# Seven block products for tiles 3 to 10 of the first feed-forward, with its modulation rows taken one token group at a time

## The chip, the cores and the metric

The kernel runs on one core of a Trainium2 chip. The metric is the device time of one execution in microseconds (us), as the median of several runs; lower is better. The profile is one further execution, taken by the hardware profiler.

The engines are named as in the profile: PE does the matrix products, DVE is the vector engine, ACT the scalar engine, POOL the general-purpose engine, SP the engine that only issues transfers. ACT can issue transfers too.

## The reference

One layer of a streaming encoder for 1024 prompt tokens and 32 sample tokens, which share all weights. The two token groups differ in the conditioning vector `c`, from which nine modulation rows of 1024 values each are made.

```python
def layer(x, c, ...):
    mod = (silu(c) @ w_ada + b_ada).reshape(B, 9, 1024)[:, None]
    modulate = lambda h, k: h * (1.0 + mod[:, :, 3*k+1]) + mod[:, :, 3*k]
    gate     = lambda k: 1.0 + mod[:, :, 3*k+2]

    f = swiglu(modulate(x, 0), ffn1_w1, ffn1_w3, ffn1_w2)      # 1024 -> 2816 -> 1024
    x = layer_norm(ALPHA * x + 0.5 * gate(0) * f, ...)
    proj = modulate(x, 1) @ w_in                               # then RG-LRU and spatial gating
    ...
    x = layer_norm(ALPHA * x + gate(1) * m, ...)
    f = swiglu(modulate(x, 2), ffn2_w1, ffn2_w3, ffn2_w2)
    x = layer_norm(ALPHA * x + 0.5 * gate(2) * f, ...)

def swiglu(h, w1, w3, w2):
    return (silu(h @ w1) * (h @ w3)) @ w2
```

So the first feed-forward needs rows 0 and 1 at its beginning (scale and shift) and row 2 (the gate) when its first result is added to `x`. Rows 3 to 8 are not needed before it ends.

## The kernel before

**Layout.** Activations lie transposed: 128 features on the partitions, tokens along the free axis, in three chunks of 384, 384 and 288 columns (`CH`). Every 32-bit operand of a matrix product is split into a rounded high part and a low rest, and a product is three matmuls: high by high, high by low, low by high. Weights are loaded by SP as 128x1024 tiles named `raw` (five buffers, 512 KB a load); ACT rounds the high part into a `wh` tile and DVE (for some pieces POOL) subtracts to get the low part. `wh` is a ring of eight. The order of all weight pieces is fixed by `stream_order`; `w_rel` hands a piece's place in the ring on as soon as PE has used it.

**The feed-forwards.** The 2816 hidden features are 22 tiles of 128, in blocks: [0, 1, 2], eight pairs [3, 4] to [17, 18], and [19, 20, 21]. For each block the hidden values g of its tiles are made first (below: H), then the down projection `F` adds all of the block's tiles to `x`. F works through its eight output tiles m, the first two together and then one by one, each with one PSUM bank per chunk (there are eight banks). `add_gated` on DVE multiplies a bank with the gate `gt` of row 2 and adds it to `x`, which also frees the bank. So a late `gt`, or a DVE that is behind, stops PE as soon as the banks are used up.

A plain tile (`H`) takes 8 input slices, 3 chunks, 2 weights (w1 and w3) and 3 matmuls each: 144 matmuls. A tile in the set `FAST` is done by `H_fast`: for the two chunks of 384 columns, the two weights and two halves of the input are taken as a 2 by 2 block product that needs seven block products in place of eight (Strassen's scheme in Winograd's form), 84 matmuls in place of 96; the third chunk stays plain (48). It pays with vector work: POOL makes four differences and sums of weight blocks per tile (in `w_source`) and splits three of the pieces, DVE adds intermediate results `y0`, `y1`, `z1` out of PSUM. A tile holds up to six PSUM banks and all five buffers `s` of intermediate values.

The seven products also need four combinations T1 to T4 of the input, once for a whole feed-forward. `combs` makes T1 and T3 (four steps of five instructions each, on POOL in the first feed-forward), then T2, which overwrites a part of the input and so waits until no plain tile needs that any more (`b12_free`); `comb_last` makes T4 behind the F that follows. T2 and T4 are made by DVE. T1 and T3 lie in the two `tx` buffers, T4 in the two `t4` buffers.

In the first feed-forward tiles 11 to 21 are fast, in the second tiles 3 to 21.

**The modulation rows.** Rows 0 and 1 are made by PE at the start. The other seven are made by `ada_rest` on DVE: per row eight weight tiles (`araw`, 128x1024), and for each of them one product with SiLU(c) of each token group (`cb`), multiplied and summed along the free axis in one instruction. A weight tile is loaded once (by SP) and used twice, first into a scratch tile `prod` (tag `acc`), then in place. The two `cb` lie in the `t4` buffers. Row 2 comes first.

**The order of work.** PE runs in program order. For DVE, ACT and POOL a scheduler orders the instructions by their place in the program and by when it reckons them ready. Side work is written as Python generators which are stepped while the matrix products are written out: `self.pe` adds up the estimated PE time (columns / 2.4 ns per matmul), and `yield 2.6` means that the generator goes on 2.6 us of PE time later. `drain` runs a generator to its end at once. `tc.issue_after(i)` puts instructions of an engine behind instruction i of that engine. Inside an engine everything runs in order: an instruction that waits holds all behind it.

`softplus` (some 30 tiny DVE instructions and one of POOL for the recurrent part) follows the first feed-forward in the program, queued behind the last instruction of the modulation rows.

Line numbers that the profile uses: L152 all matmuls; L209 and L210 high and low part of any split; L239 to L245 weight combinations on POOL; L561 and L562 other small work; L693 and L700 loads of `araw` and `cb`; L713 the modulation product; L722 `gt`; L767 to L770 the steps of T1 to T4; L817 the additions of a fast tile; L924 `add_gated`; L1160 to L1182 softplus.

Of the kernel before, what the change touches and what calls it, by code (L numbers as in the profile page):

```python
# [19 lines left out]
P = 128  # L20
# [30 lines left out]
FAST = {1: range(11, FF), 2: range(3, FF)}  # L51
# [72 lines left out]
class Core:  # L124
    def __init__(self, tc, ins, outs):
# [9 lines left out]
        self.window = False  # L135
        self.ln_out = {}
# [151 lines left out]
    def run(self):  # L288
# [396 lines left out]
    def ada_rest(self):  # L685
        nc, V = self.nc, self.nc.vector
        b_ada = self.v("b_ada").rearrange("p (m k) -> p m k", m=9)
        raws = {}

        def raw(n):  # L690
            if n < 56 and n not in raws:
                r = self.wpool.tile([P, 1024], F32, tag="raw", name="araw", bufs=RAWS)
                nc.sync.dma_start(r, self.i["ada1"][n])  # L693
                raws[n] = r


        cb = []
        for v in range(2):
            t = self.apool.tile([P, 4, 384], F32, tag="t4", name="cb", bufs=2).rearrange("p a b -> p (a b)")[:, 0:D]
            nc.sync.dma_start(t, self.i["crow"][v].partition_broadcast(P))  # L700
            nc.scalar.activation(t, t, AF.Silu)
            cb.append(t)
        raw(0)
        yield 1.0
        for m in range(2, 9):
            w = 1.8 if m == 2 else 2.6
            for f in range(K):
                n = (m - 2) * K + f
                raw(n)
                r = raws.pop(n)  # L710
                for v in range(2):
                    p = self.gpool.tile([P, D], F32, tag="acc", name="prod", bufs=1) if v == 0 else r
                    V.scalar_tensor_tensor(p, r, 1.0, cb[v], ALU.mult, ALU.mult, accum_out=self.mod[:, m, f, v:v + 1])  # L713
                    yield w
                    raw(n + 1)
            mod = self.mod[:, m, :, :]
            self.late = V.tensor_tensor(mod, mod, b_ada[:, m, :].unsqueeze(2).to_broadcast([P, K, 2]), ALU.add)
            self.mods.add(m)
            s = m // 3
            if m % 3 == 2:  # L720
                f = 0.5 if s != 1 else 1.0
                V.tensor_scalar(self.gt[:, s, :, :], mod, f, f, ALU.mult, ALU.add)  # L722
            if m % 3 == 1:
                self.coef(s, self.v("ln_g", (s - 1) * 8, s * 8), self.v("ln_b", (s - 1) * 8, s * 8), m, m - 1, 0, K)
                self.resid_coef(s, self.v("ln_g", (s - 1) * 8, s * 8), self.v("ln_b", (s - 1) * 8, s * 8))
# [20 lines left out]
    def g_tag(self, nf, t):  # L746
        return ("tx" if nf == 1 else "t4") if t == 2 else "tx" if t == LAST[2] else "g"
# [28 lines left out]
    def combs(self, e):  # L776
# [12 lines left out]
        while not self.b12_free:  # L789
            yield 1.0  # L790
        self.T2 = B12
# [10 lines left out]
    def H_fast(self, nf, t, later=False):  # L802
# [13 lines left out]
        def add(out, x, ps):  # L816
            V.tensor_tensor(out, x, ps[:, :n], ALU.add)  # L817
# [30 lines left out]
        self.w_rel(1)  # L848
        w = get("S3")
# [68 lines left out]
    def add_gated(self, ps, s, pc, m, tot=None):  # L918
# [4 lines left out]
        for (o, w, v) in segs(pc):  # L923
            V.scalar_tensor_tensor(X[:, m, a + o:a + o + w], ps[:, o:o + w], self.gt[:, s, m, v:v + 1],  # L924
                                   X[:, m, a + o:a + o + w], ALU.mult, ALU.add)
# [30 lines left out]
    def F(self, nf, block):  # L956
# [3 lines left out]
        for h in range(2):  # L960
            ws = [self.w_get((f"f{nf}w2", t, h)) for t in block]

            for ms in ((0, 1), (2,), (3,)) if h == 0 else ((0,), (1,), (2,), (3,)):
# [5 lines left out]
                for m in ms:  # L969
                    for c in range(3):  # L970
                        self.add_gated(ps[m][c], s, PIECES[c], 4 * h + m)
# [600 lines left out]
```

## Time and profile before

| | before |
|---|---|
| median of 3 runs | 1904.93 us (1904.32 to 1906.21) |
| the profiled execution | 1902.73 us |
| its span | 1901.0 us |
| mean granted PE clock | 0.991 |
| PE busy | 1847.3 us |
| DVE, ACT, POOL busy | 1257.2, 654.5, 443.7 us |
| first feed-forward, tile 1 to the F before the last block | 78 to 710 us |
| transfers | 141.08 MB, 74 GB/s over the span |
| `araw` loads | 56 of 512 KB, 3.2 us from issue to landing |
| `raw<-wst` loads (weights) | 156 of 512 KB, 3.3 us |

The span is the time from the first to the last instruction of the profiled execution; the execution's own time is 1.7 us longer. Busy times of the engines overlap, so they don't add up to the span. A row of instructions in the profile gives line, engine, operation, the tile written and the tiles read (`out<-in`), the shape, the count, and behind a bar the busy time and the mean of one; then the time that the engine stood idle before them and who ended it (`<-DMA araw<-ada` is the landing of a load).

### The profile page before, as it was taken

To read this page: it belongs to the slowest core of one execution; us is meant where nothing else is said; L and a number is where in the kernel's file an instruction comes from. 1 tells how busy PE (TensorE), PEld (TensorE's weight loads), DVE (VectorE), ACT (ScalarE), POOL (GpSimd) and SP (SyncE) were. 2 spreads that over 40 slices of the span, in tenths; PEclk is the share of its full clock that TensorE was granted. 3 is DMA by queue.
4 is the path that set the end of the run, shared out by engine and by line. 5 is a ranking of instruction groups with operands and counts; after the bars stand their busy time and mean duration, and the time that the engine had idled before them with its cause. 6 is when DMAs were issued, how large, how long until landed. Compare 5 with 4: busy or idle time off the path is not lost.

```text
span 1901.0 us, 28144 instructions
## 1 busy us (share of the span) xinstructions
PE 1847.3 (97%) x11402; PEld 1808.9 (95%) x11402; DVE 1257.2 (66%) x2307; ACT 654.5 (34%) x1144; POOL 443.7 (23%) x348
## 2 busy tenths in 40 slices
PE   6999999999999999989999999999999999999996
PEld 3899999999999999989789999999999999999996
DVE  6888878877554554873977466965645564555477
ACT  5641121112233223354554437232232233223324
POOL 2244200013233424022000000134233333423410
PEclk9999999999999999999999999999999999999998
DMA  7444344321112011222011401110121112111102
GB/s 281 145 156 135 124 152 133 123 89 41 49 45 67 23 52 60 85 77 81 3 53 45 158 23 45 45 58 32 45 67 45 45 45 67 36 54 46 45 1 92
DMA packets 39442, 141.08 MB, mean 74 GB/s; under 512 B 4368, under 2 KB 7056, under 8 KB 38544
## 3 DMA queue, kind: packets, MB, share of 16 engines
q1 hardware_dynamic: 37392, 130.03, 20.5%
q10 hardware_dynamic: 1920, 9.24, 1.2%
q8 instruction: 90, 1.47, 0.3%
q14 instruction: 40, 0.33, 0.1%
HBM read 130.52 MB, written 8.73 MB: 73 GB/s over the span
## 4 chain that ended last, share of the span: by engine, by line
PE 81%; DVE 10%; DMA 2%; ACT 1%; issue 1%; POOL 0%; POOLq 0%; DVEq 0%; ACTq 0%
PE ps L152 79%; DMA araw<-ada 2%; DVE araw L713 1%; DVE prod L713 1%; PE psl L152 1%; DVE xa L924 1%; DVE wh L210 1%; PE psz L152 1%; PE psg L152 0%; DVE g L210 0%; DVE tot L930 0%; DVE xb L1049 0%; ACT t L538 0%; DVE s L674 0%; DVE t L1060 0%
## 5 line engine op out<-in xcount | busy, mean ns | idle before, releaser
L152 PE MATMUL ps<-xh,wh 128*128 128x384 f32 (+1 forms) x4080 | 966.5, 320 | 2.3 <-ACT xh L545 1.8
L152 PEld LDWEIGHTS ps<-xh,wh 128*128 128x128 f32 x4080 | 709.4, 188 | 5.2 <-ACT xh L545 2.0
L152 PE MATMUL ps<-xl,wh 128*128 128x384 f32 (+1 forms) x2040 | 652.0, 320 | 3.3 <-DVE xl L548 3.2
L209 ACT ACTIVATE wh<-raw 128x512 fp32r<-128x512 f32 x420 | 262.1, 629 | 651.8 <-PE ps L152 553.1
L152 PE MATMUL ps<-g,wh 128*128 128x384 f32 (+1 forms) x2880 | 472.8, 324 | 4.3 <-DVE g L210 3.0
L152 PEld LDWEIGHTS ps<-g,wh 128*128 128x128 f32 x2880 | 464.0, 188 | 8.6 <-DVE g L210 4.5
L152 PEld LDWEIGHTS ps<-xl,wh 128*128 128x128 f32 x2040 | 384.2, 188 | 6.4 <-DVE xl L548 5.3
L210 DVE TENSOR_TENSOR wh<-raw,wh 128x512 fp32r<-128x512 f32 x283 | 200.4, 714 | 269.5 <-ACT wh L209 267.7
L210 POOL TENSOR_TENSOR wh<-raw,wh 128x512 fp32r<-128x512 f32 x137 | 196.2, 1433 | 331.1 <-ACT wh L209 330.8
L924 DVE SCALAR_TENSOR_TENSOR xb<-ps,gt,xb 128x384 f32<-128x384 f32 (+1 forms) x352 | 152.3, 486 | 84.9 <-PE ps L152 70.4
L924 DVE SCALAR_TENSOR_TENSOR xa<-ps,gt,xa 128x384 f32<-128x384 f32 (+2 forms) x320 | 136.6, 484 | 24.7 <-PE ps L152 24.2
L152 PE MATMUL ps<-tx,wh 128*128 128x384 f32 x720 | 129.8, 336 | 0.0
L152 PEld LDWEIGHTS ps<-tx,wh 128*128 128x128 f32 x720 | 124.3, 188 | 0.0
L209 ACT ACTIVATE g<-s 128x384 fp32r<-128x384 f32 x129 | 62.7, 493 | 170.2 <-DVE s L674 170.1
L239 POOL TENSOR_TENSOR raw<-raw 128x512 f32<-128x512 f32 x30 | 42.7, 1424 | 304.9 <-DVE wh L210 300.2
L210 DVE TENSOR_TENSOR g<-s,g 128x384 fp32r<-128x384 f32 x129 | 86.1, 674 | 20.8 <-ACT g L209 19.5
L817 DVE TENSOR_TENSOR s<-s,ps 128x384 f32<-128x384 f32 x120 | 66.3, 552 | 44.3 <-PE ps L152 44.3
L713 DVE SCALAR_TENSOR_TENSOR prod<-araw,cb 128x1024 f32<-128x1024 f32 x56 | 72.1, 1287 | 32.7 <-DMA araw<-ada 32.4
L669 ACT ACTIVATE s<-ps 128x384 f32<-128x384 f32 (+1 forms) x102 | 46.2, 453 | 120.7 <-PE ps L152 120.2
L562 POOL TENSOR_TENSOR r<-r,half 128x3 f32<-128x3 f32 x8 | 7.4, 924 | 308.1 <-DVE r L561 308.1
L713 DVE SCALAR_TENSOR_TENSOR araw<-araw,cb 128x1024 f32<-128x1024 f32 x56 | 74.2, 1325 | 1.2
L152 PE MATMUL ps<-T,wh 128*128 128x384 f32 x360 | 68.0, 337 | 0.0
(234 smaller groups left out, 1608.2 us busy)
## 6 DMA issues: line engine op xcount, KB each, us to landing
raw<-wst SPq DMA_DIRECT2D x156, 512.0 KB, 3.3
araw<-ada SPq DMA_DIRECT2D x56, 512.0 KB, 3.2
wnat<-ada SPq DMA_DIRECT2D x8, 512.0 KB, 9.9
raw<-ada SPq DMA_DIRECT2D x8, 512.0 KB, 3.4
xt<-x SPq DMA_DIRECT2D x7, 512.0 KB, 8.1
sp<-xa ACTq DMA_DIRECT2D x2, 1536.0 KB, 5.0
xb<-sp ACTq DMA_DIRECT2D x2, 1536.0 KB, 10.8
y<-xb SPq DMA_DIRECT2D x4, 768.0 KB, 3.5
```

The costliest lines, as they stand in the source:

```text
L152: self.nc.tensor.matmul(out, a, b, start=start, stop=stop, skip_group_check=True)
L209: self.nc.scalar.activation(dst_h, src, AF.Copy)
L210: (e or self.nc.vector).tensor_tensor(dst_l, src, dst_h.bitcast(F32), ALU.subtract)
L239: G.tensor_tensor(a["A21"], a["A11"], a["A21"], ALU.subtract)
L562: self.nc.gpsimd.tensor_tensor(out, out, self.half[:n, :w], ALU.pow)
L669: self.nc.scalar.activation(s, x[:, :n], AF.Silu)
L713: V.scalar_tensor_tensor(p, r, 1.0, cb[v], ALU.mult, ALU.mult, accum_out=self.mod[:, m, f, v:v + 1])
L817: V.tensor_tensor(out, x, ps[:, :n], ALU.add)
L924: V.scalar_tensor_tensor(X[:, m, a + o:a + o + w], ps[:, o:o + w], self.gt[:, s, m, v:v + 1], X[:, m, a + o:a + o + w], ALU.mult, ALU.add)
```

## The change

- `FAST` of the first feed-forward begins at tile 3, so tiles 3 to 10 take the seven products too. `combs` starts with tile 1 in place of after the first F, and its T2 steps start 3 us of PE time after `b12_free`. The hidden values of tile 2 lie in the `t4` buffers, since T1 and T3 hold `tx` already.
- `ada_rest` goes through the rows one token group at a time: row 2 with the first group, row 2 with the second, then rows 3 to 8 with the first group and again with the second. Each of the 112 products has its own load of the weight tile, and each works in place. Two `raw` buffers are held for it all along, and the loads are issued by ACT. There is only one `cb`, which is fetched and activated anew at products 0, 8, 16 and 64.
- After row 2 it pauses for 50 us of PE time. From there on a product comes every 3.8 us of PE time (before: 2.6), is queued on DVE behind the latest eviction or addition that is written out (`self.mark`), and none is written while `quiet` is set: from the S3 product of a block's last tile to the first evictions of the F behind it.
- `softplus` becomes a generator that starts 40 us of PE time after the rows are done and puts each instruction behind the latest `mark`; it is drained at the end of the first feed-forward's blocks.

```diff
-FAST = {1: range(11, FF), 2: range(3, FF)}
+FAST = {1: range(3, FF), 2: range(3, FF)}
...
         bg = self.go(self.ada_rest())
+        sp = self.go(self.softplus(bg))
         self.ffn(1, lambda: self.go(self.combs(nc.gpsimd)), bg)
         self.drain(bg)
-        with tc.issue_after(self.late.ins):
-            self.softplus()
+        self.drain(sp)
...
     def ada_rest(self):
+        todo = [(v, m, f) for ms in ((2,), range(3, 9)) for v in range(2) for m in ms for f in range(K)]
+        raws = []
+        two = [self.wpool.tile([P, 1024], F32, tag="raw", name="araw", bufs=RAWS) for _ in range(2)]
+        def raw():
+            if len(raws) < len(todo):
+                _, m, f = todo[len(raws)]
+                r = two[len(raws) % 2]
+                nc.scalar.dma_start(r, self.i["ada1"][(m - 2) * K + f])
+                raws.append(r)
+        raw()
+        raw()
+        for n, (v, m, f) in enumerate(todo):
+            if n == 16:
+                yield 50.0
+            if n in (0, 8, 16, 64):
+                cb = self.gpool.tile([P, D], F32, tag="acc", name="cb", bufs=1)
+                nc.sync.dma_start(cb, self.i["crow"][v].partition_broadcast(P))
+                yield 1.0 if n < 16 else 5.0
+                nc.scalar.activation(cb, cb, AF.Silu)
+            while self.quiet and n >= 16:
+                yield 0.5
+            with self.tc.issue_after(self.mark.ins) if n >= 16 else nullcontext():
+                V.scalar_tensor_tensor(raws[n], raws[n], 1.0, cb, ALU.mult, ALU.mult, accum_out=self.mod[:, m, f, v:v + 1])
+            yield 0.9 if n < 16 else 1.9
+            raw()
+            yield 0.9 if n < 16 else 1.9
+            if v == 1 and f == K - 1:
+                self.mod_row(m)
...
     def g_tag(self, nf, t):
-        return ("tx" if nf == 1 else "t4") if t == 2 else "tx" if t == LAST[2] else "g"
+        return "t4" if t == 2 else "tx" if t == LAST[2] else "g"
...
         while not self.b12_free:
             yield 1.0
+        yield 3.0
...
         self.w_rel(1)
+        self.quiet = any(b[-1] == t for b in BLOCKS[nf])
         w = get("S3")
...
                     for c in range(3):
                         self.add_gated(ps[m][c], s, PIECES[c], 4 * h + m)
+                self.quiet = False
...
-        if nf == 2:
-            combs = combs()
+        combs = combs()
...
-            if nf == 1 and b == BLOCKS[nf][0]:
-                combs = combs()
...
-    def softplus(self):
+    def softplus(self, bg):
+        while bg in self.side:
+            yield 10.0
+        yield 40.0
...
+        with self.tc.issue_after(self.mark.ins):
+            V.tensor_scalar(ax, lam, -1.0, None, ALU.mult)
+        yield 0.6
```

`mod_row` holds what `ada_rest` did at the end of a row (bias, `gt`, coefficients). `self.mark` is set by each addition of a fast tile (in `H_fast`) and by each `add_gated`.

More of the change, by code (lines that the diff above doesn't have):

```diff
@@ L1 @@
 import math
-from contextlib import ExitStack
+from contextlib import ExitStack, nullcontext
 import numpy as np
@@ L686, in ada_rest @@
         nc, V = self.nc, self.nc.vector
-        b_ada = self.v("b_ada").rearrange("p (m k) -> p m k", m=9)
[L688 to L725, printed above, removed]
+        todo = [(v, m, f) for ms in ((2,), range(3, 9)) for v in range(2) for m in ms for f in range(K)]
@@ L816, in add @@
         def add(out, x, ps):
-            V.tensor_tensor(out, x, ps[:, :n], ALU.add)
+            self.mark = V.tensor_tensor(out, x, ps[:, :n], ALU.add)
         k = 0 if later else 1
@@ new lines, in softplus @@
+        with self.tc.issue_after(self.mark.ins):
+            V.memset(e, math.e)
+        yield 0.6
+        with self.tc.issue_after(self.mark.ins):
+            G.tensor_tensor(z, e, ax, ALU.pow)
+        yield 0.6
+        rel = math.log(math.e) - math.log(float(np.float32(math.e)))
+        with self.tc.issue_after(self.mark.ins):
+            V.tensor_scalar(ax, ax, rel, 1.0, ALU.mult, ALU.add)
+        yield 0.6
+        with self.tc.issue_after(self.mark.ins):
+            V.tensor_tensor(z, z, ax, ALU.mult)
@@ new lines, in softplus @@
+        yield 0.6
+        with self.tc.issue_after(self.mark.ins):
+            V.tensor_scalar(s, z, 2.0, None, ALU.add)
+        yield 0.6
+        with self.tc.issue_after(self.mark.ins):
+            V.reciprocal(s, s)
+        yield 0.6
+        with self.tc.issue_after(self.mark.ins):
+            V.tensor_tensor(s, s, z, ALU.mult)
+        yield 0.6
+        with self.tc.issue_after(self.mark.ins):
+            V.tensor_tensor(q, s, s, ALU.mult)
+        yield 0.6
+        with self.tc.issue_after(self.mark.ins):
+            V.tensor_scalar(z, q, 1.0 / 17, 1.0 / 15, ALU.mult, ALU.add)
@@ new lines, in softplus @@
+        yield 0.6
+        for d in (13, 11, 9, 7, 5, 3, 1):
+            with self.tc.issue_after(self.mark.ins):
+                V.tensor_tensor(z, z, q, ALU.mult)
+            yield 0.6
+            with self.tc.issue_after(self.mark.ins):
+                V.tensor_scalar(z, z, 1.0 / d, None, ALU.add)
+            yield 0.6
+        with self.tc.issue_after(self.mark.ins):
+            V.tensor_tensor(z, z, s, ALU.mult)
+        yield 0.6
+        with self.tc.issue_after(self.mark.ins):
+            V.tensor_scalar(q, lam, -1.0, 0.0, ALU.mult, ALU.max)
@@ new lines, in softplus @@
+        yield 0.6
+        with self.tc.issue_after(self.mark.ins):
+            V.tensor_scalar(z, z, 4.0, None, ALU.mult)
+        yield 0.6
+        with self.tc.issue_after(self.mark.ins):
+            V.scalar_tensor_tensor(self.sp2, q, 2.0, z, ALU.mult, ALU.add)
+        yield 0.6
+        with self.tc.issue_after(self.mark.ins):
+            V.tensor_scalar(self.sp4, self.sp2, -2.0, None, ALU.mult)
+        yield 0.6
+        with self.tc.issue_after(self.mark.ins):
+            V.tensor_scalar(self.hb[:, 0:4], self.v("ba"), 0.5, None, ALU.mult)
@@ L1184, in sg_consts @@
+        yield 0.6
+        with self.tc.issue_after(self.mark.ins):
+            V.tensor_scalar(self.hb[:, 4:8], self.v("bx"), 0.5, None, ALU.mult)
+        yield 0.6
     def sg_consts(self):
```

38 lines of the change are left out of this document (17 added, 21 removed).

## The prediction

> **What bounds the kernel now.** I read the page's busy shares and chain first, then a table of stretches of the first feed-forward cut where the matrix products change, then what PE waited for there.
>
> ```profile
> span 1901.0 us, 28144 instructions
> ...
> PE 1847.3 (97%) x11402; PEld 1808.9 (95%) x11402; DVE 1257.2 (66%) x2307; ACT 654.5 (34%) x1144; POOL 443.7 (23%) x348
> ...
> PE 81%; DVE 10%; DMA 2%; ACT 1%; issue 1%; POOL 0%; POOLq 0%; DVEq 0%; ACTq 0%
> ```
>
> PE is busy for 97% of the span and carries 81% of the chain that ended last: what takes matrix products away shortens the kernel, as long as the other engines keep up. DVE at 66% is an average, so the stages have to be read by themselves. In the next rows H is a pair of hidden tiles, F the down projection behind it; the columns are stretch, length, busy time (and count) of each engine, granted clock, DMA share and GB/s.
>
> ```profile
> core 0: us, PE busy (x) PEld busy (x) DVE busy (x) ACT busy (x) POOL busy (x), PEclk, DMA share, GB/s
> 78.00:130.53 52.53, 50.05 (x308) 49.38 (x307) 41.98 (x65) 32.08 (x61) 17.29 (x13) 1.00 0.51 171
> 130.53:166.69 36.16, 35.20 (x218) 34.59 (x217) 35.91 (x65) 4.96 (x9) 16.74 (x12) 1.00 0.40 132
> 166.69:213.10 46.41, 46.41 (x289) 46.41 (x289) 35.10 (x54) 8.75 (x17) 22.15 (x17) 1.00 0.44 147
> 213.10:237.34 24.24, 23.78 (x146) 23.10 (x145) 24.13 (x55) 3.69 (x7) 0.00 (x0) 1.00 0.35 112
> 237.34:283.74 46.40, 46.40 (x289) 46.40 (x289) 33.04 (x60) 8.65 (x17) 0.00 (x0) 1.00 0.48 158
> 283.74:307.85 24.11, 23.52 (x146) 23.25 (x145) 23.80 (x52) 3.97 (x7) 0.00 (x0) 1.00 0.33 109
> 307.85:354.25 46.40, 46.40 (x289) 46.40 (x289) 31.59 (x60) 8.84 (x18) 0.00 (x0) 1.00 0.45 147
> 354.25:377.37 23.12, 23.12 (x146) 23.12 (x145) 22.91 (x49) 3.56 (x7) 0.00 (x0) 1.00 0.35 109
> 377.37:423.77 46.40, 46.40 (x290) 46.40 (x289) 35.53 (x87) 8.71 (x17) 5.52 (x4) 1.00 0.29 95
> 423.77:449.68 25.91, 24.08 (x147) 23.10 (x145) 25.81 (x57) 3.69 (x7) 4.66 (x4) 1.00 0.00 1
> ...
> 514.72:556.63 41.91, 41.91 (x265) 41.91 (x265) 20.25 (x33) 15.88 (x30) 14.50 (x12) 1.00 0.23 76
> 556.63:579.74 23.11, 23.11 (x145) 23.11 (x145) 15.24 (x35) 3.47 (x6) 7.51 (x6) 1.00 0.00 1
> ```
>
> The four plain pairs (tiles 3 to 10) take 46.40 us each with PE never idle; a pair of seven products (tiles 13 and 14 here) takes 41.91, also without a gap. The clock is granted in full in all of them. The F rows tell of DVE: 23.11 us where it has 15.24 us of work, but 24.24, 24.11 and 25.91 where the modulation products fill it to the brim.
>
> ```profile
> PE ps L152 <- DVE g L210: 2.5, 5, 1.1
> PE ps L152 <- ACT xh L545: 1.8, 1, 1.8
> PE ps L152 <- DVE xa L924: 1.0, 1, 1.0
> ```
>
> These are PE's three longest waits from 78 to 450 us (total, times, longest): all but the second are DVE being late at the start of an F, with the hidden values g or with the evictions xa.
>
> **The change, part by part.**
>
> *Seven products for tiles 3 to 10.* A pair loses 24 matmuls of 384 columns (289 records become 265). Four pairs by 46.40 - 41.91 = 4.49 give -18.0 us, directly on the path, since PE is the path in both kinds. What it adds to DVE, ACT and POOL stands in the fast rows already: DVE 20.25 and 15.24 us in a pair and its F.
>
> *Modulation products thinned out.* Rows 3 to 8 keep their 96 products but get a load each, and the planner's own clock (160 ns for 384 columns, 120 for 288, from the code) makes it 12 of them per pair and F, from tile 4 to tile 20, with none while the last tile's g and the first evictions are due.
>
> ```profile
> L713 DVE SCALAR_TENSOR_TENSOR prod<-araw,cb 128x1024 f32<-128x1024 f32 x56 | 72.1, 1287 | 32.7 <-DMA araw<-ada 32.4
> ...
> L713 DVE SCALAR_TENSOR_TENSOR araw<-araw,cb 128x1024 f32<-128x1024 f32 x56 | 74.2, 1325 | 1.2
> ...
> L713 DVE SCALAR_TENSOR_TENSOR prod<-araw,cb x56: 1210/1222/2028, 89.0 to 396.2; 128x1024 f32<-128x1024 f32 x56
> L713 DVE DVE_READ_ACCUMULATOR prod<-araw,cb x56: 75/82/86, 90.1 to 397.4; 128x1 f32 x56
> ```
>
> A product costs 1.31 + 0.08 = 1.39 us of DVE. In a fast pair DVE then has 20.25 + 15.24 + 12 x 1.39 = 52.2 of 65.0 us, 80%. The plain pairs of before ran at (31.59 + 22.91) / 69.5 = 78% with F at 23.12 us, at 81% with 24.11, at 84% with 24.24. So the new stall lies between 0 and 1.1 us a pair. The pause at the start of F takes the products from the place where those stalls were (g late); I take 0.3, nearest to the 78% row, for eight pairs: +2.4 us, bounds 0 and +8.8. With the same rows the old excess of the four F, 1.13 + 1.00 + 0.01 + 2.80 = 4.9 us, is gone: -4.9. Part of the 2.80 was the build-up of T2 and T4 in front of the evictions of that F; this build-up moves to the first F and is priced there.
>
> DVE beside POOL needs a price too, because seven products put the differences of weights on POOL. Two groups of the same product (count, busy us, mean ns, idle us before):
>
> ```profile
> L713 DVE SCALAR_TENSOR_TENSOR araw<-araw,cb 128x1024 f32<-128x1024 f32 x16 | 23.1, 1442 | 0.4
> ...
> L713 DVE SCALAR_TENSOR_TENSOR araw<-araw,cb 128x1024 f32<-128x1024 f32 x12 | 14.7, 1222 | 0.3
> ```
>
> The first row is the stretch 78 to 166.7 us, where POOL combines x; the second is 307.9 to 377.4, where POOL does nothing. The product costs 0.22 us more beside a POOL that is busy for two fifths of the time; in the fast pairs POOL is busy for a third (22.0 of 65.0 us), and 1.31 covers that. [...]
>
> *Row 2, and the first F.* Its gate `gt` is needed by the first eviction. Row 2 now loads each of its eight weight tiles twice, through two buffers, from ACT's queue, and fetches and activates the second `cb` in between.
>
> ```profile
> L693 SPq DMA_DIRECT2D araw<-ada x56: 327/328/328, 84.7 to 393.0; - x56
> ...
> DMA to landing us min/median/max: 3.1/3.2/4.8
> ...
> L701 ACT ACTIVATE cb<-cb x2: 1041/1052/1062, 83.1 to 84.9; 128x1024 f32<-128x1024 f32 x2
> ...
> DMA to landing us min/median/max: 3.5/3.9/4.2
> ...
> 88.96 1.23 DVE L713 SCALAR_TENSOR_TENSOR prod<-araw,cb 128x1024 f32<-128x1024 f32 x1 [0.97 <-DMA araw<-ada]
> ...
> 125.11 0.18 DVE L722 TENSOR_SCALAR gt<-mod 128x16 f32<-128x16 f32 x1
> ...
> 141.65 0.54 PE L152 MATMUL ps<-g,wh 128*128 128x288 f32 x2 [0.96 <-DVE xa L924]
> ...
> 124.93 0.63 ACT L209 ACTIVATE wh<-raw 128x512 fp32r<-128x512 f32 x1 [4.83 <-PE ps L152]
> ```
>
> Before, the first product began at 88.96 and gt was done at 125.3; PE ran out of PSUM near 140.7 and waited 0.96 us. After, a buffer's round is 1.39 + 0.33 + 3.2 = 4.9 us for two products in turn, 16 of them 39 us, and the new `cb` 0.3 + 3.9 + 1.05 = 5.3 us: gt at about 89 + 39 + 5.3 + 0.6 = 134, in time. With every landing at 4.8 and one load queued on ACT behind a weight copy that waits 4.83 us for PE (last row), it is 89 + 52 + 5.3 + 0.6 + 4.8 = 152: 11 us late. In the same F the 14 products that DVE did before (20 us of its 35.91) make room for T2 and part of T4. The second feed-forward does just that:
>
> ```profile
> 1212.73:1247.66 34.93, 34.93 (x219) 34.79 (x217) 32.69 (x72) 4.96 (x9) 10.77 (x7) 1.00 0.00 1
> ```
>
> Its first F takes 34.93 us with both builds in it, against 36.16 here. So this part lies between -1.2 and +11. T1 and T3 now go to POOL during the plain tiles 1 and 2; before, they filled most of POOL's 17.29, 16.74 and 22.15 us in the first three rows of the table, some 53 us, so begun at 78 they end near 135, and the first fast tile wants them at 167. I take +2 us: gt in time, but DVE with a backlog of g, T2 and evictions.
>
> *Loads on ACT.* 112 issues at 0.33 us put 37 us on ACT, which is idle for 45 us of each 65; they leave SP, where only weight loads remain. DMA traffic for the modulation doubles in bytes, but 12 loads of 512 KB in 65 us are 97 GB/s, and with the weights (76 GB/s over H, none over F) 146: no more than the 147 to 158 of the plain pairs. Nothing, unless ACT is held: the rival below. The four `cb` fetches stay on SP and wait there for the last product of the old `cb`; the weight loads behind them are a dozen pieces ahead.
>
> *softplus.* By the planner's clock it falls in one lump behind tile 20, and it takes 7 us of DVE there:
>
> ```profile
> 403.19 0.16 DVE L1160 TENSOR_SCALAR spt<-vec 128x4 f32<-128x4 f32 x1
> ...
> 410.00 0.17 DVE L1180 TENSOR_SCALAR sp<-sp 128x4 f32<-128x4 f32 x1
> ```
>
> Tile 21's seven products give DVE 13 us before its g is wanted, so most of it is covered; with an early hiccup of ACT at the first loads I take +0.6 (0 to 3).
>
> **Sum.** -18.0 - 4.9 + 2.4 + 2.0 + 0.6 = -17.9 us. The profiled execution took 1902.7 (span 1901.0), so 1884.8 for one like it; the median of the three runs is 2.2 above it, 1904.9, and there the forecast is 1887.0. What a measurement can tell from no change is about 0.2%, 3.8 us.
>
> **The rivals.**
>
> *Half is given back.* Stalls of the 84% row in all eight pairs (+8.8) or a late gt (+11) in place of my 2.4 or 2.0: 1893 to 1901. For it: POOL beside DVE, and 32.4 us that DVE already stood waiting for loads. Against it: the pair at 78% without a gap, and the pause.
>
> *ACT or DVE stands in the chain of every fast tile.* A fast tile has steps ACT, DVE, ACT between its products, and one product or one waiting load in front of them costs 1.39 us. If that reached PE in each of the 16 tiles, +22 in place of the 2.4: about 1907, no change. [...] Against it: six PSUM banks of eight are taken by a tile, and a step has the next two products of 12 matmuls, 1.9 us each, to finish.
>
> *Row 2 far too late: slower.* If the two buffers did not overlap (each load issued only when ACT comes round, each product in order behind it), a product would cost 1.39 + 0.33 + 4.8 = 6.5 us, gt would come at 89 + 104 + 6 = 199, and PE would stand for 58 us: about 1943. The change turns slower once gt is later than about 162, some 4.2 us per product. Against it: before, eight loads and 16 products took 36 us, 4.5 us a load.
>
> **How the numbers follow.** Forecast (1881 to 1893) 0.66; half given back 0.18; no gain, 1907, 0.08, of which 0.06 within 0.2%; row 2 late 0.05; more than 24 us gained 0.03. Lowest sum: -18.0 - 4.9 - 1.2 = -24.1, 1880.8. The range is 1881 to 1898, into the first rival. Faster 0.87, same 0.06, slower 0.07.
>
> **What would show it.** Pairs of tiles 3 to 10 at 41.9 us and their F near 23.1; gt before 141 and the first F at 36 to 39; 12 products per pair at 1.3 us; PE's waits on g and xa no longer than before. A first F beyond 45 us, pairs above 43, or ACT waiting for DVE at its load issues would make the prediction wrong.

## The result, and the profile after

The changed kernel takes 1895.65 us (median of 4 runs, 1893.90 to 1897.66), the kernel before 1905.57 us beside it (1904.32 to 1908.11): a ratio of 0.9948, 95% interval 0.9932 to 0.9964, some 10 us less. The forecast was 1887.0. The profiled execution took 1897.66 us against 1902.73, so the two traces differ by only 5.1 us: that of after lies 2.0 above its median, that of before 2.8 below.

The page of after, span and busy shares (lines move by two to twenty: the matmuls are L154, the low part of a split L212, the modulation product L715, `gt` L731, the steps of T1 to T4 L776 to L779, `add_gated` L935):

```profile
span 1895.9 us, 28268 instructions
...
PE 1833.2 (97%) x11306; PEld 1796.3 (95%) x11306; DVE 1316.9 (69%) x2347; ACT 682.3 (36%) x1194; POOL 547.8 (29%) x412
```

PE lost only 14 us of busy time. The same stretches as before, cut where H and F change (first F, then the pairs of tiles 3 to 12 with their F):

```profile
129.28:175.35 46.07, 37.77 (x219) 37.08 (x217) 42.37 (x78) 6.65 (x11) 21.60 (x16) 0.89 0.26 84
175.35:217.26 41.91, 41.91 (x266) 41.91 (x266) 32.63 (x52) 15.08 (x30) 14.92 (x12) 1.00 0.30 101
217.26:240.37 23.11, 23.11 (x146) 23.11 (x146) 20.28 (x43) 3.47 (x6) 7.11 (x6) 1.00 0.20 69
240.37:282.28 41.91, 41.91 (x265) 41.91 (x265) 31.15 (x49) 15.73 (x30) 16.45 (x11) 1.00 0.58 189
282.28:305.59 23.31, 23.31 (x145) 23.21 (x145) 20.51 (x43) 3.47 (x6) 7.32 (x6) 1.00 0.20 68
...
435.66:477.66 42.00, 42.00 (x265) 41.86 (x265) 27.12 (x41) 14.97 (x28) 14.85 (x11) 1.00 0.56 188
477.66:506.21 28.55, 25.47 (x145) 24.79 (x145) 24.15 (x49) 4.84 (x9) 8.74 (x7) 0.94 0.16 56
506.21:548.14 41.93, 41.93 (x265) 41.93 (x265) 30.74 (x49) 15.39 (x30) 17.15 (x11) 1.00 0.58 189
548.14:571.93 23.79, 23.38 (x145) 23.11 (x145) 21.33 (x48) 3.64 (x7) 7.27 (x6) 1.00 0.20 67
```

Two rows stand out. The first F takes 46.07 us, 9.9 more than before, and the F of tiles 11 and 12 takes 28.55, 5.4 more than its neighbours. In both PE was idle (8.3 and 3.1 us) and the granted clock fell (0.89 and 0.94). The other pairs run close to the forecast: 41.91 to 42.00 us, and an F of 23.11 to 23.79. DVE is busy for 81% of the first pair with its F (32.63 + 20.28 of 65.0), where F takes 23.11, and for 79% of the second (31.15 + 20.51 of 65.2), where it takes 23.31. PE's two longest waits from 78 to 790 us name the two places:

```profile
PE ps L154 <- DVE gt L212: 7.5, 1, 7.5
PE ps L154 <- ACT g L211: 2.5, 1, 2.5
```

The first is not a wait for the gate: `gt` at L212 is the low part of tile 2's hidden values, which lie in the `t4` buffers under that name. The time line of DVE around it (start, length, what; in brackets the idle time before):

```profile
135.97 0.44 DVE L676 TENSOR_TENSOR s<-s,ps 128x288 f32<-128x288 f32 x1
138.02 0.56 DVE L776 TENSOR_TENSOR s<-tx,xh 128x384 f32<-128x384 f32 x1 [1.60 <-POOL s L777]
138.49 1.52 DVE L715 SCALAR_TENSOR_TENSOR araw<-araw,cb 128x1024 f32<-128x1024 f32 x1
...
139.95 1.47 DVE L212 TENSOR_TENSOR wh<-raw,wh 128x512 fp32r<-128x512 f32 x1
141.34 1.21 DVE L715 SCALAR_TENSOR_TENSOR araw<-araw,cb 128x1024 f32<-128x1024 f32 x1
...
142.48 2.44 DVE L212 TENSOR_TENSOR gt<-s,gt 128x384 fp32r<-128x384 f32 x3
...
147.95 0.17 DVE L731 TENSOR_SCALAR gt<-mod 128x16 f32<-128x16 f32 x1
```

Between the last multiplication of tile 2 (135.97) and its low parts (142.48) stand the first instruction of T2 (L776), which waits 1.60 us for POOL's T3, two products of row 2 and a split of weights. The gate itself comes at 148.0, 23 us later than before, but after PE has started again. What PE does meanwhile:

```profile
136.20 0.44 PE L154 MATMUL ps<-gt,wh 128*128 128x384 f32 x1
```

That is its first matmul with the high part of tile 2's hidden values, ready before the low part; the next, which needs the low part, comes after the wait, and 17 of them take 5.33 us, nearly twice the usual time (the row of 30 in the last section):

```profile
144.14 5.33 PE L154 MATMUL ps<-gt,wh 128*128 128x384 f32 x17 [7.51 <-DVE gt L212]
```

The first F is longer than before by 7.3 us of idle PE (8.3 in place of 1.0 in the stretches) and 2.6 us of half clock (37.8 us busy in place of 35.2). The chain of waits from 125 to 176 us by line, in which POOL's steps of T1 and T3 stand ahead of DVE's:

```profile
by line: PE ps L154 62.5%; POOL s L777 9.4%; POOL s L776 8.3%; POOL tx L779 5.9%; POOL tx L778 4.4%; issue 3.8%; DVE araw L715 3.2%; DVE gt L212 3.0%; DVE wh L212 2.7%; DVE s L776 0.1%; DVEq L212 0.0%
```

In the F of tiles 11 and 12 the time line of ACT shows what came in between:

```profile
466.88 1.06 ACT L711 ACTIVATE cb<-cb 128x1024 f32<-128x1024 f32 x1 [3.65 <-DMA cb<-crow]
...
476.17 0.64 ACT L211 ACTIVATE wh<-raw 128x512 fp32r<-128x512 f32 x1 [2.70 <-DMA raw<-wst]
...
482.93 0.63 ACT L211 ACTIVATE wh<-raw 128x512 fp32r<-128x512 f32 x1 [1.94 <-POOL raw L243]
```

It is the fetch of the other group's `cb` at product 64: ACT's activation stands in front for 3.65 us until it has landed, so ACT copies weights later, the loads into their buffers come later, and the last SiLU of tile 12 (at 483.46, right behind the last row) is late for F. SP is not what held the loads: the fetch stood 2.0 us on SP for the last product of the old `cb`, but the load behind it (461.0) had to wait for POOL's last split of its buffer in any case (459.4 to 460.9).

### The profile page after: what moved, and what is told of

It is laid out like the page before. It is cut to its first block, busy times and chain, and to the rows that moved or that the text cites. A ratio compares the mean times of both kernels' runs of the same rounds, so it can differ in the third digit from the quotient of the medians.

```text
span 1895.9 us, 28268 instructions
## 1 busy us (share of the span) xinstructions
PE 1833.2 (97%) x11306; PEld 1796.3 (95%) x11306; DVE 1316.9 (69%) x2347; ACT 682.3 (36%) x1194; POOL 547.8 (29%) x412
## 4 chain that ended last, share of the span: by engine, by line
PE 85%; DVE 8%; POOL 3%; ACT 2%; DMA 1%; issue 1%; SPq 0%; POOLq 0%; DVEq 0%; ACTq 0%
PE ps L154 82%; PE psl L154 1%; DVE xl L550 1%; POOL s L776 1%; DVE wh L212 1%; PE psz L154 1%; POOL tx L779 1%; PE psa L154 1%; POOL s L777 1%; DMA raw<-wst 1%; DVE araw L715 1%; PE psg L154 0%; ACT t L540 0%; POOL tx L778 0%; DVE tot L941 0%
## 5 line engine op out<-in xcount | busy, mean ns | idle before, releaser
L154 PE MATMUL ps<-xh,wh 128*128 128x384 f32 (+1 forms) x3824 | 902.0, 319 | 2.3 <-ACT xh L547 1.8
L154 PEld LDWEIGHTS ps<-xh,wh 128*128 128x128 f32 x3824 | 662.7, 188 | 5.3 <-ACT xh L547 2.0
L154 PE MATMUL ps<-xl,wh 128*128 128x384 f32 (+1 forms) x1912 | 609.0, 319 | 4.3 <-DVE xl L550 4.2
L154 PE MATMUL ps<-g,wh 128*128 128x384 f32 (+1 forms) x2808 | 462.7, 325 | 4.8 <-ACT g L211 2.5
L154 PEld LDWEIGHTS ps<-g,wh 128*128 128x128 f32 x2808 | 455.2, 189 | 7.8 <-ACT g L211 3.0
L212 DVE TENSOR_TENSOR wh<-raw,wh 128x512 fp32r<-128x512 f32 x283 | 216.8, 771 | 244.4 <-ACT wh L211 242.4
L154 PEld LDWEIGHTS ps<-xl,wh 128*128 128x128 f32 x1912 | 360.0, 188 | 7.8 <-DVE xl L550 6.5
L212 POOL TENSOR_TENSOR wh<-raw,wh 128x512 fp32r<-128x512 f32 x169 | 251.8, 1492 | 392.9 <-ACT wh L211 392.7
L935 DVE SCALAR_TENSOR_TENSOR xb<-ps,gt,xb 128x384 f32<-128x384 f32 (+1 forms) x352 | 152.2, 486 | 85.1 <-PE ps L154 70.8
L154 PE MATMUL ps<-tx,wh 128*128 128x384 f32 x912 | 164.5, 336 | 0.0
L715 DVE SCALAR_TENSOR_TENSOR araw<-araw,cb 128x1024 f32<-128x1024 f32 x112 | 153.7, 1373 | 13.2 <-DMA araw<-ada 11.3
L241 POOL TENSOR_TENSOR raw<-raw 128x512 f32<-128x512 f32 x38 | 54.7, 1440 | 360.3 <-DVE wh L212 351.6
L154 PEld LDWEIGHTS ps<-tx,wh 128*128 128x128 f32 x912 | 157.3, 188 | 0.1
L935 DVE SCALAR_TENSOR_TENSOR xa<-ps,gt,xa 128x384 f32<-128x384 f32 (+1 forms) x320 | 136.1, 482 | 7.4 <-PE ps L154 7.0
L211 ACT ACTIVATE g<-s 128x384 fp32r<-128x384 f32 (+1 forms) x126 | 61.2, 493 | 156.5 <-DVE s L676 156.5
L212 DVE TENSOR_TENSOR g<-s,g 128x384 fp32r<-128x384 f32 (+1 forms) x126 | 94.8, 759 | 22.1 <-ACT g L211 21.2
L154 PE MATMUL ps<-T,wh 128*128 128x384 f32 x456 | 86.2, 337 | 0.0
L243 POOL TENSOR_TENSOR raw<-raw 128x512 f32<-128x512 f32 x38 | 57.0, 1501 | 95.5 <-DVE wh L212 91.4
L676 DVE TENSOR_TENSOR s<-s 128x384 f32<-128x384 f32 x76 | 58.8, 774 | 32.5 <-ACT s L877 31.4
```

The costliest lines, as they stand in the source:

```text
L154: self.nc.tensor.matmul(out, a, b, start=start, stop=stop, skip_group_check=True)
L211: self.nc.scalar.activation(dst_h, src, AF.Copy)
L212: (e or self.nc.vector).tensor_tensor(dst_l, src, dst_h.bitcast(F32), ALU.subtract)
L241: G.tensor_tensor(a["A21"], a["A11"], a["A21"], ALU.subtract)
L243: G.tensor_tensor(a["A22"], a["A22"], a["A21"], ALU.subtract)
L676: self.nc.vector.tensor_tensor(s, s, x, ALU.mult)
```

## The experiments

**e1: no refetch at product 64.** All rows of the second group take the first group's `cb`.

```diff
-            if n in (0, 8, 16, 64):
+            if n in (0, 8, 16):
```

> The changed kernel without the second fetch of cb at product 64 (rows 3 to 8 of the second token group then use the first group's cb). In the changed kernel the F of tiles 11 and 12, just after this fetch, took 28.7 us in place of 23.3. Theory: the SiLU of the new cb stands in ACT's queue 3.65 us until the fetch has landed, the weight copies behind it free their raw buffers late, and the weight loads and tile 12's g come late: this F goes back to 23.3 to 23.5 us and the time falls by 5 us to about 1890.5. Rival: DVE at 80% with products in between stalls now and then, and the fetch has no part in it: that F stays at 27 us or more, or another one takes its place, and the time stays within 1.5 us of 1895.6.

Measured: 1890.28 us, ratio 0.9905 (0.9889 to 0.9921). The F of tiles 11 and 12:

```profile
476.62:499.73 23.11, 23.11 (x145) 23.11 (x145) 20.29 (x43) 3.47 (x6) 7.11 (x6) 1.00 0.21 69
```

As the theory had it, the 5.4 us are the refetch: ACT copies its next two weights at 462.3 and 463.3 in place of 467.9, though this F begins only 1.1 us earlier. All eight F of the pairs now lie within 0.1 us of 23.11. The first F keeps its length (46.65).

**e2: no refetch at product 8.** Row 2 of the second group takes the first group's `cb`.

```diff
-            if n in (0, 8, 16, 64):
+            if n in (0, 16, 64):
```

> The changed kernel without the second fetch of cb at product 8 (row 2 of the second group then uses the first group's cb). In the changed kernel the first F took 46.2 us, 10 more than before, PE waiting 7.5 us in it for the low part of tile 2's g, behind row 2's last products on DVE; row 2 ended at 147. Theory: row 2 as rebuilt (16 loads on ACT and a second cb) is too long; without the second cb it ends some 5 us earlier, and the first F takes 40 to 42 us. Rival: POOL's T1 and T3 steps, moved beside row 2, stretch DVE's instructions; the fetch only fills time in which DVE had other work: the first F changes by less than 2 us.

Measured: 1895.95 us, 0.9941 (0.9918 to 0.9964); first F 47.0, `gt` at 146.8. One `cb` fetch less in row 2 changes nothing that can be told, so the theory fails and the rival holds.

**e3: no products for row 2.** Its loads and its two fetches of `cb` go with them; its gate is made of the bias alone, and rows 3 to 8 start at the same place of the plan.

```diff
-        todo = [(v, m, f) for ms in ((2,), range(3, 9)) for v in range(2) for m in ms for f in range(K)]
+        todo = [(v, m, f) for ms in (range(3, 9),) for v in range(2) for m in ms for f in range(K)]
...
+        V.memset(self.mod[:, 2, :, :], 0.0)
+        self.mod_row(2)
+        yield 81.0
```

> The changed kernel without row 2's 16 products and loads (the gate row is set to its bias alone), the rest of the modulation at the same planned times. Theory, row 2 holds tile 2's g on DVE: the first F falls from 46.2 to 35 to 36.5 us, the time by some 10 us, to about 1886. Rival, the T2 steps, which wait for POOL, stand before tile 2's g: the first F stays above 41 us.

Measured: 1885.21 us, 0.9879 (0.9858 to 0.9900). The first F:

```profile
132.80:170.50 37.70, 35.28 (x218) 34.64 (x217) 32.11 (x66) 4.84 (x9) 9.36 (x7) 1.00 0.00 0
```

With T1, T2 and T3 all there it takes 37.7 us and keeps its clock (1.00). Row 2 is needed for the loss. The total hits the forecast of 1886 in part by luck: the first F gives 8.4 us and the F of tiles 11 and 12 another 5.0 (23.6 here, with its refetch), while the first F begins 3.5 us later.

**e4: T1 and T3 with two of POOL's five instructions per step** (their values are not the combinations).

```diff
+        if e is self.nc.gpsimd:
+            e.tensor_copy(dst[0][:, k, :], x[0][:, k, :].bitcast(F32))
+            e.tensor_tensor(dst[1][:, k, :], y[0][:, k, :].bitcast(F32), dst[0][:, k, :].bitcast(F32), ALU.subtract)
+            return
```

> The changed kernel with two of the five POOL instructions of each T1 and T3 step of the first feed-forward (T1 and T3 are then copies, not differences), so that POOL is done with them after some 20 us. Theory, POOL beside row 2 stretches DVE's products (1.5 to 2.08 us in place of 1.22) and splits: row 2 ends at 138 to 141 in place of 147, and the first F takes 37 to 40 us. Rival, row 2 is bound by its loads, the second cb and ACT's queue: row 2 ends after 144, and the first F stays above 43 us.

Measured: 1895.37 us, 0.9933 (0.9910 to 0.9956). The products are at 1.22 us again, yet `gt` comes at 147.0: DVE waited 10.8 us for loads. The first F took 36.6 us but began at 138.0, 8.7 us later than after; row 2's first product already began 6.5 us later (95.3 in place of 88.8). For the total that is inconclusive: a gain in one place and a loss in the other. For the price it isn't: between row 2's first and last product DVE was busy for 50.1 of 58.1 us in after, with POOL busy for 52.3, and for 32.8 of 51.0 us here, with POOL busy for 1.5.

**e5: row 2 in pairs.** Eight loads, each used for both groups, with both `cb` held (`acc` and a `t4` buffer); rows 3 to 8 as changed.

```diff
...
+        for f in range(K):
+            r = raws[f]
+            V.scalar_tensor_tensor(prod, r, 1.0, cbs[0], ALU.mult, ALU.mult, accum_out=self.mod[:, 2, f, 0:1])
+            yield 1.8
+            V.scalar_tensor_tensor(r, r, 1.0, cbs[1], ALU.mult, ALU.mult, accum_out=self.mod[:, 2, f, 1:2])
+            yield 0.9
+            raw()
+            yield 0.9
+        self.mod_row(2)
+        yield 55.0
...
```

> The changed kernel with row 2 done as before the change: eight loads, each used for both token groups, with both cb at hand (the second in a t4 buffer, the scratch product in the other); rows 3 to 8 one group at a time as in the changed kernel, cb fetched anew only at the middle of them. Theory, the doubled loads and the slower plan of row 2 are what makes it late: row 2 ends at 128 to 135 in place of 147, beside the same POOL work, the first F takes 36 to 38.5 us in place of 46.1, and the time falls by 8 to 10 us to about 1886.5. Rival, POOL's steps beside it: row 2 ends after 141, the first F stays above 42 us, and the time above 1892.

Measured: 1898.46 us, 0.9967 (0.9952 to 0.9981). The gate is done at 134.8, as wanted, but the first F takes 53.2 us. DVE's time line:

```profile
133.83 0.92 DVE L752 TENSOR_SCALAR gt<-mod 128x16 f32<-128x16 f32 x1
140.43 0.56 DVE L797 TENSOR_TENSOR s<-tx,xh 128x384 f32<-128x384 f32 x1 [5.68 <-POOL s L798]
142.45 0.56 DVE L797 TENSOR_TENSOR s<-tx,xl 128x384 f32<-128x384 f32 x1 [1.47 <-POOL tx L800]
...
147.84 1.38 DVE L676 TENSOR_TENSOR s<-s,ps 128x384 f32<-128x384 f32 x3
```

DVE is idle for 5.7 us with a step of T2 (L797 here) at the head of its queue; the multiplications of tile 2, whose SiLU is done at 132.6, come behind two steps of T2 and the start of a third, at 147.8, and PE waits 14.7 us. Both the theory and the rival fail: row 2 is early, and the first F is longer than in any run so far. The length of row 2 alone is not the cause.

**e6: e5, and the refetch's activation 7 us later in a fixed place.**

```diff
-                yield 5.0
-                i = nc.scalar.activation(cb, cb, AF.Silu)
+                yield 12.0
+                i = nc.scalar.activation(cb, cb, AF.Silu)
+                self.tc.keep_in_program_order(i)
```

> The kernel of the run before (row 2 in pairs), and the one refetch of cb with 12 us of plan in place of 5 between fetch and SiLU, the SiLU pinned behind all that ACT was given until then. Theory: the F of tiles 11 and 12 is back at 23.1 to 23.5 us, all F of the pairs together have no more than 1 us over 23.11 each, and the time is 1880 to 1883, ratio to the kernel before 0.986 to 0.988. Rival, the refetch holds ACT wherever its SiLU stands: some F is still 26 us or more, and the time stays within 2 us of that run.

Measured: 1899.34 us, 0.9962 (0.9948 to 0.9976); first F 53.3, the same wait of 14.7 us, so the theory's 1880 to 1883 us fail. All F of the pairs are 23.11 here, but they are in e5 too, so the later place isn't shown to be needed. Where the refetch falls to tiles 11 and 12 (the changed kernel and its variants but e1 and e8), the loss goes with the time for which the activation stands in ACT's queue: where it waited 0 to 2.7 us for the fetch (e3, e5, e6, e7, e9, e12) the F of tiles 11 and 12 took 23.1 to 23.6 us, where it waited 3.65 to 4.48 us (after, e2, e4, e10) it took 27.7 to 28.6.

**e7: the loads of `araw` on SP** in place of ACT.

```diff
-                nc.scalar.dma_start(r, self.i["ada1"][(m - 2) * K + f])
+                nc.sync.dma_start(r, self.i["ada1"][(m - 2) * K + f])
```

> The changed kernel with all loads of the modulation weights issued by SP in place of ACT. Theory, ACT's queue is not what makes row 2 late (its waits behind the loads fall mostly on the residual activations, which nobody waits for): row 2 ends within 3 us of 147, the first F stays within 2 us of 46, the time within 2 us of 1895.6. Rival, a load that waits for its product holds ACT, and ACT the high part of tile 2's g: row 2 ends before 142, and the first F takes less than 42 us.

Measured: 1907.04 us, 0.9998 (0.9987 to 1.0010): the whole gain is gone. First F 52.0, and four of the eight F of the pairs 25.1, 27.1, 24.4 and 25.2. PE's waits from 78 to 790 us:

```profile
PE ps L154 <- DVE s L676: 15.5, 1, 15.5
PE ps L154 <- ACT g L211: 3.2, 4, 1.2
PE ps L154 <- DVE g L212: 2.2, 4, 0.6
```

Loads issued by ACT are the better choice of the two as the kernel stands. But part of the loss is not SP's: in this run the scheduler put the first steps of T2 ahead of tile 2's multiplications, as in e5. DVE stood 4.0 us until 139.95 for POOL's T3, and the multiplications came at 147.89. Neither the theory nor the rival had this.

**e8: the new modulation alone**, tiles 3 to 10 plain.

```diff
-FAST = {1: range(3, FF), 2: range(3, FF)}
+FAST = {1: range(11, FF), 2: range(3, FF)}
```

> The changed kernel with tiles 3 to 10 plain again, so the new modulation alone. Theory: the pairs 3 to 10 take 46.4 us again, 18.0 us more in sum; their F take 23.1 to 23.4, but the last of them, with T2 and T4, 24 to 26; the first F stays at 43 to 46 us, since row 2 is late without any fast tile: 1910 to 1914, slower than the kernel before. Rival, the T2 and T4 steps in the first F are what makes it long: it takes 36 to 39 us here, and the time is 1902 to 1906.

Measured: 1913.98 us, 1.0041 (1.0024 to 1.0058), slower than before, as the theory had it. The plain pairs take 46.4 us again, so the seven products are worth their 18 us. The first F takes 43.1 us with T2 not there yet (it is made behind tile 10 here, where its steps stand ahead of that tile's multiplications on DVE, and that F takes 29.8 in place of the theory's 24 to 26): row 2, with T1 and T3 on POOL, gives some 7 of the 9.9 us without T2; e10 puts 2 us on T2's place.

**e9: e6, with T2 behind tile 2's hidden values.** `split` returns its instruction; `glu_end` keeps it as `g_last`.

```diff
-            self.comb(self.T2, ALU.add, self.T3, B11, k, V)
+            with self.tc.issue_after(self.g_last.ins):
+                self.comb(self.T2, ALU.add, self.T3, B11, k, V)
```

> The kernel of e6 (row 2 in pairs with both condition rows held, refetch's activation pinned 12 us on) with one more edit: the DVE steps of T2 are issued after the low part of tile 2's last hidden value. In e5 and e6 PE stood 14.7 us for DVE's multiplication of tile 2; DVE itself was idle from 134.8 to 140.4 with a step of T2 at the head of its queue, which needs POOL's T3. Theory (T2 at the head of DVE's queue, behind POOL's T3, is what holds tile 2): the multiplications follow row 2's last step at about 134, the wait falls from 14.7 to under 3 us, no or one window at half clock, first F 36 to 39, pairs' F 23.1 each, T2 still ready before tile 3 at about 170: 1881 to 1885 in place of 1899. Rival (DVE is held by something else there, a split of wh or POOL's weights, and T2 only stands ahead of it): the wait stays over 8 us, first F over 45, 1893 or more. Second rival: T2 now comes late and tile 3 waits for it: first F short, but a new wait on a T2 step at the first pair, 1886 to 1892.

Measured: 1891.76 us, 0.9917 (0.9903 to 0.9931); first F 46.5. PE's waits from 78 to 790 us:

```profile
PE ps L154 <- DVE xa L957: 4.7, 1, 4.7
PE ps L154 <- DVE s L676: 2.2, 1, 2.2
```

The 14.7 us in front of tile 2 fell to 2.2, as the theory said, but the first F and the total did not follow it: a new wait of 4.7 us stands for `add_gated` (L957). DVE there:

```profile
143.65 0.56 DVE L797 TENSOR_TENSOR s<-tx,xh 128x384 f32<-128x384 f32 x1 [0.91 <-POOL s L798]
145.71 1.63 DVE L797 TENSOR_TENSOR s<-tx,xl 128x384 f32<-128x384 f32 x1 [1.50 <-POOL tx L800]
...
150.62 1.68 DVE L957 SCALAR_TENSOR_TENSOR xa<-ps,gt,xa 128x384 f32<-128x384 f32 x4
```

T2's steps now hold the evictions in place of tile 2. The total lies 7.6 us below e6; the first F got 6.9 us shorter.

**e10: the changed kernel with that one edit** to T2, row 2 and the refetch as they are.

> The changed kernel with only the edit on T2: its DVE steps are issued after tile 2's last hidden value; row 2's sixteen products with one condition row, and the refetch, stay as they are. In the changed kernel DVE waits 1.6 us in T2's first step at 136.4 to 138.0, and that step and one product stand ahead of tile 2's low parts. Theory (both are needed: row 2's length pushes DVE's work to 148, T2's order adds to it): the 7.5 us wait falls by 2 to 4 us, first F 42 to 45, 1891 to 1894. Rival (T2's order alone is the cause): the wait is gone, first F 36 to 39, 1885 to 1888. Rival (row 2's length alone): the wait stays at 7 to 8, first F 45 to 47, 1894 to 1897.

Measured: 1894.37 us, 0.9933 (0.9920 to 0.9947); first F 44.1.

```profile
PE ps L154 <- DVE gt L212: 5.5, 2, 3.6
PE ps L154 <- ACT g L211: 2.5, 1, 2.5
```

The wait falls from 7.5 to 5.5 us in two parts: the 2 us that T2's first instruction cost (1.60 of waiting and 0.56 of work) are gone, row 2's are left. The refetch's 2.5 us stand as before. That is the theory's size, with the first F inside its range; in the total the edit isn't told from after.

**e11: the kernel before again.**

> The kernel before once more, for a second profile: the mixing stage took 402.7 us in the profile before and 404.8 to 405.7 in all profiles with the new modulation. If that is a property of the new kernels, this one is 402 to 403 again, with 13 to 14 us of half clock there; if it is the phase of the throttle's windows, it may be anywhere from 402.5 to 406, with more half clock where it is longer.

Measured: 1903.29 us, one run. The mixing stage (all that lies between the two feed-forwards) took 404.3 us here and 402.7 in the first profile, with PE 392.2 us busy and a granted clock of 0.98 in both. So 1.6 of the 2.8 us by which the mixing stage of after exceeds the first profile lie within what the kernel before does by itself; after's PE is 393.5 us busy there at a clock of 0.97. The profiles with the new modulation have 404.2 to 405.7; whether a microsecond of that belongs to the change stays open. Neither alternative of the expectation fits: the stage was longer here with no more half clock. The first F took 37.4 us here, against 36.2 in the first profile, and began at 128.4 against 130.5. So of the 9.9 us some 1.2 lie within the spread of the kernel before, and the 37.7 us of e3 are within 0.3 us of its own second profile.

**e12: e6, with T2 later** and behind the sums of `add_gated`.

```diff
-        yield 3.0
+        yield 16.0
...
-            self.comb(self.T2, ALU.add, self.T3, B11, k, V)
+            with self.tc.issue_after(self.mark.ins):
+                self.comb(self.T2, ALU.add, self.T3, B11, k, V)
```

> The kernel of e6 with T2 16 us later than its present place and each of its DVE steps issued after the gated sums written before it (L957), in place of e9's place right behind tile 2's hidden values. In e9 T2's steps stood in front of the first gated sums, two of them waited for POOL (T3 is done at 145.7 there), the sums started at 150.6 and PE waited 4.7 us for the PSUM banks that they free. Theory (a T2 step at the head of DVE's queue before POOL has T3 holds whatever stands behind it): here five groups of sums stand ahead of T2, T3 is done by 146 to 148, so nothing is held; remaining waits of PE 1 to 3 us for the multiplication of tile 2, first F 36 to 39, pairs' F 23.1 each, tile 3 not late, total 1881 to 1885. Rival (row 2 in pairs leaves DVE and ACT so late that the first F is long anyway): first F over 43, 1889 to 1893. Rival (T2 or T4 is late for tile 3): first F short, but PE waits on a T2 or T4 step in the first pair for more than 3 us, 1885 to 1890.

Measured: 1892.02 us, 0.9928 (0.9915 to 0.9941). The first F and the H of tiles 3 and 4:

```profile
129.30:169.31 40.01, 36.79 (x219) 36.23 (x218) 32.75 (x61) 6.27 (x12) 22.08 (x19) 0.96 0.12 40
169.31:216.51 47.20, 43.58 (x266) 43.26 (x266) 38.81 (x66) 15.65 (x30) 15.07 (x12) 0.96 0.31 101
```

The first F falls from 53.3 to 40.0 us, just short of the theory's 36 to 39, but the pair of tiles 3 and 4 pays 5.3 us, of which ACT's time line shows the beginning:

```profile
179.90 0.49 ACT L856 ACTIVATE s<-ps 128x384 f32<-128x384 f32 x1 [2.35 <-DVE T L800]
```

ACT's first copy of tile 3 waits for DVE's steps of T4: both take their intermediate values from the five `s` buffers. So the second rival of that run held in kind: late vector work moved from one place to the next.

## Why the prediction was right in direction and range, and half off in size

The forecast was a gain of 17.9 us, the measured one is 9.9, in the place of the rival "half is given back" (1893 to 1901; by its own prices one of its two losses alone gives 1893 or 1896, both together 1902). The range held because it reached into this rival, which is in part luck: the rival's late gate came, but the full stalls in all eight pairs did not, and one of the two real losses, the refetch, had no price at all. By the prediction's own signs the first F was wrong: it named a first F beyond 45 us (46.07 here) and wanted the gate before 141 (148.0). By its terms:

- *Seven products, -18.0:* right. Four H by 46.40 - 41.91 in the rows, and e8 loses the 18 us again.
- *Old excess of four F, -4.9:* right for those four (23.11 to 23.31 now).
- *Stalls in the pairs, +2.4:* came out as +6.3: 0.2, 0.7 and 5.4. The stall of a DVE at 80% came out smaller than the 0.3 us taken (81% with an F of 23.11, 79% with 23.31). What failed is the sentence that priced the four `cb` fetches at nothing, because "the weight loads behind them are a dozen pieces ahead". It looked at SP's queue only; the activation that follows waits on ACT's queue for the landing, in front of ACT's weight copies (e1).
- *Row 2 and the first F, +2.0 (bounds -1.2 to +11):* came out as +9.9, near the upper bound. The backlog of DVE that the term names is what came; its size was wrong, and three things failed in it. The first is the price of DVE's work: 1.31 us for a product (1.39 with the reading of its sum), where beside POOL's T1 and T3 it took 1.75 on average. These products and their loads follow as a group of 16 from 85 to 148 us:

```profile
L715 DVE SCALAR_TENSOR_TENSOR araw<-araw,cb 128x1024 f32<-128x1024 f32 x16 | 27.9, 1748 | 6.4 <-DMA araw<-ada 4.6 <-ACT cb L711 1.8
```

  The prediction had signs of it at hand, 1.44 us on average from 78 to 167 us before and 2.03 at the longest, and set them aside. The 16 products make up 7 of the 14 us by which row 2 was late (148 in place of 134, 4 us before the far bound). Much of the rest is DVE's other work between them, which the sum of loads and buffers left out: the ten splits of weights in this stretch took 1.40 us each, against 0.89 beside row 2 before, and DVE was busy for 50.1 of 58.1 us. The second is the wrong consumer: the working asked when the gate would be late for the first eviction; PE stopped earlier, at the hidden values of tile 2, which stand behind row 2's products in DVE's queue. The third is that T2's first steps were counted as DVE work, not as a wait: they need POOL's T3, which by the estimate was done near 135 and in the trace only at 140.9, and whatever the scheduler puts behind them waits with them (e5, e9).
- *Clock, not priced:* each of the two stalls cost its length and then matmuls at a granted clock of 0.50, 2.6 us in the first F and 2.4 in the other (PE 25.47 us busy where its neighbours have 23.11).
- *softplus and start, +0.6:* no stall behind the rows can be put to it; the last pairs' F take 23.11.

In the traces: first F +9.9, its start -1.3, H -17.9, F of the eight pairs +1.4, mixing stage +2.8, second feed-forward -0.1, before rounding together -5.1, the difference of the spans. The 4.8 us between this and the 9.9 of the medians are the place of the two profiled executions within their spread; no stage of the traces can account for them.

The rival that ACT or DVE stands in the chain of every fast tile is refuted by the H rows of 41.91. That a load which waits holds ACT's work behind it does show, in the waits of ACT from 78 to 150 us:

```profile
ACT xa L558 <- DVE araw L715: 10.0, 5, 5.3
...
ACT gt L211 <- DVE araw L715: 3.9, 1, 3.9
```

ACT's next work waited, up to 5.3 us, for a product of DVE that the load in front of it was waiting for. It costs PE nothing in the pairs, whose H rows stay at 41.91 to 42.00 us.

What is shown: the refetch, by the wait of its activation (e1, and the comparison in e6), row 2's part in the first F (e3, e8), T2 holding whatever stands behind it in DVE's queue (its waits for POOL: 5.68 and 1.47 us in e5, 0.91 and 1.50 in e9, 1.60 in after, against which PE's wait in e10 is 2.0 shorter), and DVE's work taking longer beside POOL's steps (1.75 us a product in after, 1.22 in e4). Not shown: a version without either loss. e9 and e12 leave nothing out and have the lowest times of such kernels, 1891.8 and 1892.0 us (ratios to before 0.9917 and 0.9928, after 0.9948, the intervals of e9 and after just apart), but each turned the wait of the first F into another one; the 37.7 us of e3 weren't reached with row 2 in place. How much of the first F is POOL's alone stays open, since e4 also changed what came before.

## What to carry to other kernels

Price moved work on every in-order queue that it touches, by what stands behind it there: here an instruction that waited (a step that needs another engine's result, 5.68 us in e5; an activation that needs a fetch, 3.65 us in after) cost its wait to the first urgent instruction behind it, however little work it was itself (0.56 and 1.06 us). Ask which consumer comes first, not only which one the moved result has. And where such a step is pushed back, look at what the same buffers and the same engine are needed for next: here the wait moved there, 4.7 us for `add_gated` in e9 and 3.6 us for tile 3 in e12.

## What the runs showed of the hardware that wasn't expected

Stalls of PE cost more than their length. After 7.5 us of waiting the next 17 matmuls took 314 ns each (5.33 / 17) at a granted clock of 0.50, where 30 in a row at full clock take 169:

```profile
477.67 5.06 PE L154 MATMUL ps<-g,wh 128*128 128x384 f32 x30
```

The time at half clock came in multiples of about 3.4 us: 10.24 in the first F of after (139.17 to 149.41 us), 3.41 in the F of tiles 11 and 12 (from 487.33). Between the two the clock was full for 337.92 us, which is 99 pieces of 3.413, so both stretches lie on one grid of such pieces. PE was not idle for a whole piece ahead of every stretch: in the F of tiles 11 and 12 of after the two waits below, with 1.89 us of idle PE in the piece from 483.92 to 487.33, were enough for 3.41 us at half clock, and in the first F of e12 PE was idle for only 3.2 us in all (40.01 less 36.79) and the granted clock was 0.96.

```profile
485.26 0.44 PE L154 MATMUL ps<-g,wh 128*128 128x384 f32 x1 [2.54 <-ACT g L211]
486.25 20.13 PE L154 MATMUL ps<-g,wh 128*128 128x384 f32 x113 [0.55 <-DVE g L212]
```

Not every wait did this. The one of 1.8 us near 80 us, for ACT's `xh`, left the clock at 1.00 before and after. What separates them is the idle share of one such piece of 3.41 us. From 60 to 830 us of the traces of before and after PE was idle for 1.60 to 2.53 us of the piece ahead of each of the five stretches at half clock, and for at most 1.56 us of any piece between two at full clock. So in these two traces the limit lies near 1.6 us, about half a piece, with the reserve that the ends of matmuls in a trace are modelled. Inside a stretch it doesn't hold: from 818.43 us in after PE had no idle time for a piece, and the next piece was at 0.50 too.
